# All projections of h ahead of the retention, by seven block products for eight, with results kept in DRAM and low halves made by adding DMAs

## The chip, the cores and the metric

The kernel runs on one core of a Trainium2 chip. The metric is the device time in microseconds of one execution; lower is better. Engine names are those of the profile: PE (TensorE, matmuls), DVE (VectorE), ACT (ScalarE), POOL (GpSimd), SP (SyncE, which here issues nearly all DMAs).

## The reference, cut to what matters

One decoder layer for 1024 tokens of width 1024, batch 1, depth 1, all in f32:

```
mod = c @ w_ada + b_ada;  shift, scale, gate = split(mod, 3)
h = rmsnorm(x, pre_norm_g) * (1 + scale) + shift
q, k, v, z_ret, u_val, u_gate, z_conv, g_a, g_b = split(h @ w_in)   # 1024, 1024, 2048, 2048, then five of 1024
q, k = rotary(q), rotary(k) / 16                                    # 4 heads of 256
ret = head_groupnorm(retention_chunkwise(q, k, v))                  # 4 heads, v of 512 a head, decay per head
y_a = (ret * silu(z_ret)) @ w_ret_out
a = causal_depthwise_conv(u_val * sigmoid(u_gate), 31 taps)
y_b = (silu(layernorm(a)) * silu(z_conv)) @ w_conv_out
y = (sigmoid(g_a) * y_a + sigmoid(g_b) * y_b) @ w_out
out = x + gate * rmsnorm(y, post_norm_g)
```

## The kernel before

**Precision.** Each f32 operand of a large matmul is split into two float32r tiles: hi, a rounded copy made on ACT, and lo = src - hi, made on DVE (`split`, L124). A product is then three matmuls: hi x hi, hi x lo, lo x hi (`mm3`, L142). One matmul is 128 x 128 weights by up to 512 columns; a projection of 256 channels over all tokens (`proj_T` on the two halves of a `load_chunk`) is 2 x 2 tiles x 8 slices of the contraction x 3 = 96 matmuls.

**Block products.** `strassen` (L220) does the same 256 x 1024 x 1024 block with seven products of 12 matmuls, for eight. It needs sums of the weights, which `load_s` (L193) makes on DVE for each block (x1, x2, wa, then splits), and sums of h (T1 to T4), which `sums_of` (L664) makes once. Four copies of PSUM (p1, p5, u2, u3) go through ACT, three sums through DVE, and a callback gets each 128 x 512 result. Weights come through `wst` (two buffers of 512 KB) and their halves through `whl` (three pairs).

**Stages.** First mod, then `make_h` (h transposed to channels x tokens, in hi and lo, 16 tiles). Three `u_chunk`s (u_gate, u_val, plain) store a to DRAM and queue the convolution: 8 x 30 taps on DVE, each over 1024 tokens, put in by `pump` between matmul tiles at a lowered priority (`LATER`). Then q and k of head 0, the last `u_chunk`, and for each head plain q and k projections with the rotary on DVE (`rot_proj`), scores, the v projection token-major (`wide_proj`), states and outputs with a group norm, o kept in DRAM (o_d). After the heads come the sums T1 to T4, beside one plain block of g_a (`PLAIN`), and then block products of z (eight, with o read back and transposed by PE), g_a (three), g_b (four) with the layer norm's statistics, and z_conv (four). Results go to DRAM (r_d, sga_d, sgb_d, b_d). Last, three parts of output projection (two of w_ret, one of w_conv), then w_out, the norm and the residual.

**Order of the work.** The program is unrolled; a scheduler orders each engine's instructions ahead of time, by priority in program order, with its own estimate of durations. At run time each engine's queue, the DMA queue of SP among them, is worked off in order. Buffers come from pools: `unit` (38 tiles of 512 KB), `LD` (three), `TMP` (nine), PSUM (eight banks).

Of the kernel before, what the change touches and what calls it, by code (L numbers as in the profile page):

```python
# [26 lines left out]
PLAIN = 1  # L27
# [42 lines left out]
def block_kernel(ctx: ExitStack, tc: tile.TileContext, x, c, positions, w_ada, w_in, w_ret_out, w_conv_out,  # L70
# [68 lines left out]
    def load_chunk(w, c0, half=0):
        return [load_w(w, half + i, c0 // 256) for i in range(2)]  # L140
# [8 lines left out]
    def proj_T(ch, src, cb, th, name):  # L149
        ps = PS(name)  # L150
        pairs = []
        for k in range(4 * len(ch)):
            hi, lo = ch[k // 4]
            cs = slice(cb * P, cb * P + P)
            ts = slice(th * 512, th * 512 + 512)
            pairs.append(((hi[:, k % 4, cs], lo[:, k % 4, cs]), (src[k][0][:, ts], src[k][1][:, ts])))
        mm3(ps, pairs, True, True)
        return ps

    def load_wide(w, c0, qk):  # L160
        hi, lo = load_w(w, qk % 2, c0 // 256 + qk // 2)
        return [t.rearrange("p (k x) n -> p k (x n)", x=2) for t in (hi, lo)]
# [18 lines left out]
    def proj_group(ch, src, tiles, name):  # L181
        pss = [PS(name) for _ in tiles]
        for k in range(KK):
            hi, lo = ch[k // 4]
            for ps, (cb, th) in zip(pss, tiles):
                cs = slice(cb * P, cb * P + P)
                ts = slice(th * 512, th * 512 + 512)
                mm3(ps, [((hi[:, k % 4, cs], lo[:, k % 4, cs]), (src[k][0][:, ts], src[k][1][:, ts]))],
                    k == 0, k == KK - 1)
        return pss  # L190


    def load_s(w, ci):  # L193
        st = []
        for half in range(2):
            st.append(wst.tile([P, 4, 256], F32, name="ws", tag="ws"))
            nc.sync.dma_start(out=st[half], in_=w[ci, half])
        n0, n1 = slice(0, P), slice(P, 256)
        a11, a21, a12, a22 = st[0][:, :, n0], st[0][:, :, n1], st[1][:, :, n0], st[1][:, :, n1]
        wa = wst.tile([P, 2, 4, P], F32R, name="wa", tag="wa", bufs=1)  # L200
        split(a11, wa[:, 0], wa[:, 1], V)
        x1 = LD("x1").rearrange("p (k n) -> p k n", n=256)
        V.tensor_tensor(out=x1[:, :, n0], in0=a21, in1=a22, op=ALU.add)
        V.tensor_tensor(out=x1[:, :, n1], in0=x1[:, :, n0], in1=a11, op=ALU.subtract)
        x2 = LD("x2").rearrange("p (k n) -> p k n", n=256)
        V.tensor_tensor(out=x2[:, :, n0], in0=a12, in1=x1[:, :, n1], op=ALU.subtract)
        V.tensor_tensor(out=x2[:, :, n1], in0=a11, in1=a21, op=ALU.subtract)
        res = []
        for x in (x1, x2, st[1]):
            hi = whl.tile([P, 4, 256], F32R, name="wh", tag="wh")  # L210
            lo = whl.tile([P, 4, 256], F32R, name="wl", tag="wl")
            split(x, hi, lo, V)
            res.append((hi, lo))
        sets = {"11": (wa[:, 0], wa[:, 1])}
        for names, (hi, lo) in zip((("S1", "S2"), ("S4", "S3"), ("12", "22")), res):
            for j, name in enumerate(names):
                sets[name] = (hi[:, :, j * P:(j + 1) * P], lo[:, :, j * P:(j + 1) * P])
# [65 lines left out]
    wg0 = load_chunk(w_in, UG0)  # L283
# [65 lines left out]
    cout_d = [dram.tile([P, 1024], F32, name=f"cout_d{i}") for i in range(8)]  # L349
    a_d = [dram.tile([P, 1024], F32, name=f"a_d{i}") for i in range(8)]  # L350
    csum_d = dram.tile([P, 1024], F32, name="csum_d")
    mb_d = [dram.tile([P, 1024], F32, name=f"mb_d{i}") for i in range(8)]
    r_d = [dram.tile([P, 1024], F32, name=f"r_d{i}") for i in range(16)]
    csum = U(name="csum")

    ln_tasks = []

    def conv_tasks(i):
# [16 lines left out]
        def end():  # L375
            nc.sync.dma_start(out=cout_d[i], in_=st["o"])
            if i == 0:
                V.tensor_copy(out=csum, in_=st["o"])
            else:
                V.tensor_tensor(out=csum, in0=csum, in1=st["o"], op=ALU.add)  # L380

        bgq.append((1.0, begin))
        for s_ in range(1, CW):
            bgq.append((1.7, lambda s_=s_: tap(s_)))
        bgq.append((0.0, end))
        if i == 7:
            bgq.append((0.0, lambda: nc.sync.dma_start(out=csum_d, in_=csum)))
# [37 lines left out]
    def trig_begin():  # L425
        posi = U(I32, name="posi")
# [40 lines left out]
    bgp.append((4.0, trig_begin))  # L467
    for j, (src, n, red) in enumerate((("a1", 0, 1), ("a1", 1, 1), ("a2", 0, 1), ("a1", 2, 0), ("a2", 1, 0),
                                       ("a1", 3, 0), ("a2", 2, 0))):
        bgp.append((3.5 if red else 1.2, lambda src=src, n=n, red=red, j=j: turns(src, n, red, j == 0)))  # L470
# [3 lines left out]
    def u_chunk(ci):  # L474
        wg = load_chunk(w_in, UG0 + 256 * ci) if ci else wg0
        sg = {}
        for th in range(2):
            if ci == 0:
                make_h(th)
            pss = proj_group(wg, hT, [(0, th), (1, th)], "pg") if ci == 0 else None  # L480
            for cb in range(2):
                ps = pss[cb] if ci == 0 else proj_T(wg, hT, cb, th, "pg")
                sg[cb, th] = TMP(name="sg")
                A.activation(out=sg[cb, th], in_=ps, func=AF.Sigmoid)
                if ci or (cb and th):
                    pump(5.0, 4.0)
        wv = load_chunk(w_in, UV0 + 256 * ci)
        for cb in range(2):
            a = U(name="a")
            for th in range(2):  # L490
                ps = proj_T(wv, hT, cb, th, "pu")
                V.tensor_tensor(out=a[:, th * 512:(th + 1) * 512], in0=ps, in1=sg[cb, th], op=ALU.mult)
                pump(4.4, 4.0)
            nc.sync.dma_start(out=a_d[2 * ci + cb], in_=a)
            conv_tasks(2 * ci + cb)

    for ci in range(3):
        u_chunk(ci)
    while "cos" not in tr:
        pump(0.0, 5.0)  # L500
    sinT, cosT = tr["sin"], tr["cos"]


    def rot_proj(h, c0):
        ch = load_chunk(w_in, c0 + 256 * h)
        res, kf = [], []
        for th in range(2):
            sl = slice(th * 512, (th + 1) * 512)
            p1 = proj_T(ch, hT, 0, th, "pq1")
            p2 = proj_T(ch, hT, 1, th, "pq2")  # L510
            t_a, t_b, t_c, t_d = TMP(name="ta"), TMP(name="tb"), TMP(name="tcc"), TMP(name="td")
            if c0 == K0:
                kf.append(U(F32, (P, 2, 512), "kf"))
                f_a, f_c = kf[th][:, 0, :], kf[th][:, 1, :]
            else:
                f_a, f_c = t_a, t_c
            V.tensor_tensor(out=t_a, in0=p1, in1=cosT[:, sl], op=ALU.mult)
            V.tensor_tensor(out=t_c, in0=p1, in1=sinT[:, sl], op=ALU.mult)
            V.tensor_tensor(out=t_b, in0=p2, in1=sinT[:, sl], op=ALU.mult)
            V.tensor_tensor(out=t_d, in0=p2, in1=cosT[:, sl], op=ALU.mult)  # L520
            V.tensor_tensor(out=f_a, in0=t_a, in1=t_b, op=ALU.subtract)
            V.tensor_tensor(out=f_c, in0=t_c, in1=t_d, op=ALU.add)
            hi = U(F32R, (P, 2, 512), "qkh")
            lo = U(F32R, (P, 2, 512), "qkl")
            split(f_a, hi[:, 0, :], lo[:, 0, :], V)
            split(f_c, hi[:, 1, :], lo[:, 1, :], V)
            res.append((hi, lo))
            pump(3.8, 3.0)
        return (res, kf) if kf else res

    qk0 = (rot_proj(0, Q0), rot_proj(0, K0))
    u_chunk(3)

    o_d = [dram.tile([P, 8, 512], F32, name=f"o_d{i}") for i in range(H)]
    for h in range(H):
        q, kT = (rot_proj(h, Q0), rot_proj(h, K0)) if h else qk0
        kT, kf = kT

        kna = (U(F32R, (P, 4, 256), "knh"), U(F32R, (P, 4, 256), "knl"))
        knb = U(F32R, (P, 4, 256), "knx")  # L540
        kn = [(kna[0][:, t, :], kna[1][:, t, :]) if t < 4 else (knb[:, t - 4, :], knb[:, t - 2, :]) for t in range(6)]
# [415 lines left out]
```

## Time and profile before

| | us |
|---|---|
| median of 3 runs | 1488.21 (1486.33 to 1491.5) |
| the profiled execution | 1492.43 |
| its span | 1490.7 |
| PE busy | 1447.0 |
| DVE busy | 1045.2 |
| ACT busy | 466.1 |
| POOL busy | 48.6 |

The span runs from the first to the last instruction of the profiled execution; the rest of its time lies around it. Busy times are of one engine each and overlap one another. A matmul's recorded duration overlaps that of the next, since the engine is pipelined: the distance between starts is what one costs. The granted clock (PEclk) is TensorE's share of its full 2.4 GHz in a stretch.

### The profile page before, as it was taken

To read this page: it belongs to the slowest core of one execution; us is meant where nothing else is said; L and a number is where in the kernel's file an instruction comes from. 1 tells how busy PE (TensorE), PEld (TensorE's weight loads), DVE (VectorE), ACT (ScalarE), POOL (GpSimd) and SP (SyncE) were. 2 spreads that over 40 slices of the span, in tenths; PEclk is the share of its full clock that TensorE was granted. 3 is DMA by queue.
4 is the path that set the end of the run, shared out by engine and by line. 5 is a ranking of instruction groups with operands and counts; after the bars stand their busy time and mean duration, and the time that the engine had idled before them with its cause. 6 is when DMAs were issued, how large, how long until landed. Compare 5 with 4: busy or idle time off the path is not lost.

```text
span 1490.7 us, 16850 instructions
## 1 busy us (share of the span) xinstructions
PE 1447.0 (97%) x6648; PEld 1193.9 (80%) x6648; DVE 1045.2 (70%) x1374; ACT 466.1 (31%) x696; POOL 48.6 (3%) x69
## 2 busy tenths in 40 slices
PE   6799999999999999999899999999899999999998
PEld 2688888888888888888688888888688888888888
DVE  5869899998697688589889855497955244464335
ACT  2612112132223213222543434454744021122121
POOL 2200000001001001000000000000000000000001
PEclk9899999999999999999899999999999999999999
DMA  9122222212102202121454533466636344353402
GB/s 370 58 100 84 72 71 85 85 57 85 57 29 99 71 29 86 44 70 43 171 171 143 185 97 104 149 205 199 216 124 237 107 160 152 112 190 121 154 29 114
DMA packets 61665, 176.39 MB, mean 118 GB/s; under 512 B 6417, under 2 KB 14737, under 8 KB 61586
## 3 DMA queue, kind: packets, MB, share of 16 engines
q1 hardware_dynamic: 61298, 175.14, 34.8%
q8 instruction: 52, 0.85, 0.2%
q14 instruction: 27, 0.22, 0.0%
q10 hardware_dynamic: 288, 0.17, 0.0%
HBM read 132.30 MB, written 42.99 MB: 118 GB/s over the span
## 4 chain that ended last, share of the span: by engine, by line
PE 87%; DVE 8%; DMA 2%; issue 1%; ACT 1%; POOL 0%; SPq 0%; DVEq 0%; POOLq 0%; ACTq 0%
PE pya L145 6%; PE pya L146 6%; PE pya L147 6%; PE pza L226 6%; PE pq L145 4%; PE pq L147 4%; PE pq L146 4%; PE pv L147 3%; PE pv L145 3%; PE pv L146 3%; PE pzc L226 3%; PE pgaa L226 2%; PE pzca L226 2%; PE py L145 2%; PE py L146 2%; PE py L147 2%
## 5 line engine op out<-in xcount | busy, mean ns | idle before, releaser
L371 DVE SCALAR_TENSOR_TENSOR co<-ca,vec,co 128x1023 f32<-128x1023 f32 (+16 forms) x240 | 303.0, 1266 | 3.6
L125 ACT CAST wh<-ws 128x1024 fp32r<-128x1024 f32 x101 | 106.3, 1052 | 374.7 <-PE pya L146 119.3
L126 DVE TENSOR_TENSOR wl<-ws,wh 128x1024 fp32r<-128x1024 f32 x97 | 118.4, 1222 | 102.6 <-ACT wh L125 99.4
L146 PE MATMUL pya<-rl,wh 128*128 128x512 f32 x384 | 149.4, 390 | 0.0
L145 PE MATMUL pya<-rh,wh 128*128 128x512 f32 x384 | 149.0, 391 | 0.0
L147 PE MATMUL pya<-rh,wl 128*128 128x512 f32 x384 | 148.5, 390 | 0.0
L146 PE MATMUL pv<-wl,hh 128*128 128x512 f32 x256 | 99.8, 390 | 0.0
L147 PE MATMUL pv<-wh,hl 128*128 128x512 f32 x256 | 99.8, 392 | 0.0
L146 PE MATMUL pq<-hl,wh 128*128 128x512 f32 x256 | 99.7, 390 | 0.0
L145 PE MATMUL pq<-hh,wh 128*128 128x512 f32 x256 | 99.7, 390 | 0.0
L145 PE MATMUL pv<-wh,hh 128*128 128x512 f32 x256 | 99.4, 390 | 0.0
L147 PE MATMUL pq<-hh,wl 128*128 128x512 f32 x256 | 99.1, 390 | 0.0
L145 PEld LDWEIGHTS pya<-rh,wh 128*128 128x128 f32 x384 | 72.1, 188 | 15.1 <-ACT wh L125 0.2
L146 PEld LDWEIGHTS pya<-rl,wh 128*128 128x128 f32 x384 | 72.1, 188 | 15.1 <-issue 0.2
L147 PEld LDWEIGHTS pya<-rh,wl 128*128 128x128 f32 x384 | 72.1, 188 | 15.0
L146 PE MATMUL py<-wl,mh 128*128 128x256 f32 (+1 forms) x192 | 61.0, 319 | 0.0
L147 PE MATMUL py<-wh,ml 128*128 128x256 f32 (+1 forms) x192 | 61.0, 319 | 0.0
L145 PE MATMUL py<-wh,mh 128*128 128x256 f32 (+1 forms) x192 | 60.6, 319 | 0.0
L226 PE MATMUL pza<-T,wh 128*128 128x512 f32 x192 | 60.2, 395 | 0.0
L852 DVE TENSOR_TENSOR ya<-pya,gld 128x512 f32<-128x512 f32 x32 | 22.1, 690 | 53.9 <-PE pya L147 53.9
L147 PEld LDWEIGHTS pq<-hh,wl 128*128 128x128 f32 x256 | 48.1, 188 | 10.0
L145 PEld LDWEIGHTS pq<-hh,wh 128*128 128x128 f32 x256 | 48.1, 188 | 9.9
(338 smaller groups left out, 3181.0 us busy)
## 6 DMA issues: line engine op xcount, KB each, us to landing
ws<-in_w_in SPq DMA_DIRECT2D x88, 512.0 KB, 3.6
ada<-in_w_ada SPq DMA_DIRECT2D x16, 512.0 KB, 10.2
o_d<-o SPq DMA_DIRECT2D x16, 512.0 KB, 2.6
oc<-o_d SPq DMA_DIRECT2D x16, 512.0 KB, 5.3
ws<-in_w_ret_out SPq DMA_DIRECT2D x16, 512.0 KB, 4.4
rld<-r_d SPq DMA_DIRECT2D x16, 512.0 KB, 4.6
gld<-sga_d SPq DMA_DIRECT2D x16, 512.0 KB, 4.2
x<-in_x SPq DMA_DIRECT2D x8, 512.0 KB, 10.2
```

The costliest lines, as they stand in the source:

```text
L125: A.copy(out=hi, in_=src)
L126: lo_eng.tensor_tensor(out=lo, in0=src, in1=f(hi), op=ALU.subtract)
L145: T.matmul(ps, a[0], b[0], start=start and i == 0, stop=False)
L146: T.matmul(ps, a[0], b[1], start=False, stop=False)
L147: T.matmul(ps, a[1], b[0], start=False, stop=stop and i == n - 1)
L226: T.matmul(ps, l_[:, k, :], r_, start=start and k == 0 and i == 0, stop=k == 3 and i == 2, skip_group_check=True)
L371: V.scalar_tensor_tensor(out=st["o"][:, s_:], in0=st["a"][:, 0:1024 - s_], scalar=vec[:, i, ROW_CW + k:ROW_CW + k + 1], in1=st["o"][:, s_: ...
L852: V.tensor_tensor(out=y, in0=ps, in1=gld[:, sl], op=ALU.mult)
```

## The change

All 44 blocks of h @ w_in but the first of u_gate and u_val go through `strassen`, in one stage ahead of everything else; `sums_of` therefore runs right after h. q, k (after the rotary), v, silu(z) and the gates are stored in DRAM (q_d, k_d, v_d, sz_d, sga_d, sgb_d). v comes out channels x tokens. The convolution's taps, angles and layer norm are pumped between the products. Retention follows in 16 steps (4 heads x 4 chunks of 256 tokens): `fetch` reads a chunk's q, k and v, splits them and transposes k and v by PE, one step ahead; `scores`, `state` and `outputs` hold the same matmuls as before; `gated` transposes o, multiplies by silu(z) and stores r_d. Between the steps stand the 16 tiles of y_b (`conv_out`, 24 matmuls each), which were the third part of the output projection. The two parts of w_ret stay at the end.

Most low halves of weights are now made by `split_dma`: ACT writes hi and then lo = -hi, and a DMA from POOL's queue adds the source to lo, from DRAM again or from the tile in SBUF. `split` on DVE stays for x2, for what is read back, and for plain blocks. The convolution's sum over channels (csum) is made by adding DMAs in DRAM. Weights are laid out by the host so that blocks are contiguous. `whl` has four pairs for three, `unit` 36 for 38. In the first step `make_h` does the second half of the tokens first.

```diff
-    unit = ctx.enter_context(tc.tile_pool(name="unit", bufs=38))
+    unit = ctx.enter_context(tc.tile_pool(name="unit", bufs=36))
     wst = ctx.enter_context(tc.tile_pool(name="wst", bufs=2))
-    whl = ctx.enter_context(tc.tile_pool(name="whl", bufs=3))
+    whl = ctx.enter_context(tc.tile_pool(name="whl", bufs=4))
...
+    def split_dma(src, hi, lo, again):
+        A.copy(out=hi, in_=src)
+        A.activation(out=lo, in_=f(hi), func=AF.Copy, scale=-1.0)
+        G.dma_start(out=lo, in_=again, accum_op=ALU.add)
...
-        split(a11, wa[:, 0], wa[:, 1], V)
...
+        split_dma(a11, wa[:, b0], wa[:, b1], w[ci, 0][:, b0])
...
+        for names, x, again in ((("S1", "S2"), x1, x1), (("S4", "S3"), x2, None), (("12", "22"), st[1], w[ci, 1])):
+            hi = whl.tile([P, 1024], F32R, name="wh", tag="wh")
+            lo = whl.tile([P, 1024], F32R, name="wl", tag="wl")
+            if again is None:
+                split(x, hi, lo, V)
+            else:
+                split_dma(x, hi, lo, again)
...
             if i == 0:
-                V.tensor_copy(out=csum, in_=st["o"])
+                G.dma_start(out=csum_d, in_=st["o"])
             else:
-                V.tensor_tensor(out=csum, in0=csum, in1=st["o"], op=ALU.add)
+                G.dma_start(out=csum_d, in_=st["o"], accum_op=ALU.add)
...
+    sg = [U(name="sg") for _ in range(2)]
+    for th in (1, 0):
+        make_h(th)
+        pss = proj_group(wg0, hT, [(0, th), (1, th)], "pg")
         for cb in range(2):
...
+            evac_pg(sg)(cb, th, pss[cb], None)
...
+    wv0 = load_chunk(w_in, UV0 // 256)
     for k in range(4):
         sums_of(k)
...
+    for th in (1, 0):
+        for cb in range(2):
+            evac_pu(0, sg)(cb, th, proj_T(wv0, hT, cb, th, "pu"), TMP(name="pu"))
...
+    ws_ = load_s(w_in, UG0 // 256 + 1)
     for k in range(4):
         split(t1s[k // 2][:, k % 2, :], *hT2["T1"][k], V)
...
+    def qk_group(h, c0, dst):
+        ws_ = load_s(w_in, c0 // 256 + h)
+        outs = {}
...
+            if cb == 0:
+                o = outs[th] = U(F32, (P, 2, 512), "qk")
+                V.tensor_tensor(out=o[:, 0, :], in0=src, in1=tr["cos"][:, sl], op=ALU.mult)
+                V.tensor_tensor(out=o[:, 1, :], in0=src, in1=tr["sin"][:, sl], op=ALU.mult)
+                return
+            o = outs[th]
+            t1 = TMP(name="rt")
+            V.tensor_tensor(out=t1, in0=src, in1=tr["sin"][:, sl], op=ALU.mult)
+            V.tensor_tensor(out=o[:, 0, :], in0=o[:, 0, :], in1=t1, op=ALU.subtract)
+            V.tensor_tensor(out=t, in0=src, in1=tr["cos"][:, sl], op=ALU.mult)
+            V.tensor_tensor(out=o[:, 1, :], in0=o[:, 1, :], in1=t, op=ALU.add)
+            nc.sync.dma_start(out=dst[h][:, :, sl], in_=o)
...
+        strassen(ws_, hT2, "pq", evac, lambda: pump(0.6, 0.6))
...
+    u_groups(1, ws_)
+    u_groups(2)
+    u_groups(3)
...
     for h in range(H):
...
+        qk_group(h, Q0, q_d)
+        g_group(GA0, h, sga_d)
+        qk_group(h, K0, k_d)
+        g_group(GB0, h, sgb_d)
+        for cv in range(2):
+            v_group(h, cv)
+        if h < 2:
+            for cz in range(2):
+                z_group(h, cz)
+    for cz in range(2):
+        z_group(2, cz)
+    pump(1e9, 1e9)
...
+    bgp.append((3.5, ln_rstd))
+    bgp.append((2.0, ln_spread))
+    for i in range(2):
+        bgp.append((1.0, lambda i=i: b_load(i)))
+    for cz in range(2):
+        z_group(3, cz)
     pump(1e9, 1e9)
...
+    def fetch(s):
+        h, n = s // NCH, s % NCH
...
+        split(raw, d["hi"], d["lo"], V)
...
+        vh, vl = U(F32R, (P, 2, 512), "vh"), U(F32R, (P, 2, 512), "vl")
+        for b in range(2):
+            ps = PS("vt")
+            for e in range(4):
+                T.transpose(ps[:, e * P:(e + 1) * P], vr[:, e, b * P:(b + 1) * P], ident)
...
+    def conv_out(j):
+        th, ci, cb = j // 8, (j % 8) // 2, j % 2
+        if cb == 0:
+            wc["ch"] = load_chunk(w_conv, ci, by_dma=True)
...
+        mm3(ps, pairs, True, True)
+        V.tensor_tensor(out=t, in0=ps, in1=t, op=ALU.mult)
+        nc.sync.dma_start(out=mb_d[2 * ci + cb][:, halves[th]], in_=t)
...
+    fetch(0)
+    for s in range(NS + 1):
+        if s < NS:
+            scores(s)
+            if s + 1 < NS:
+                fetch(s + 1)
+            if s % NCH < NCH - 1:
+                state(s)
+        if s in (0, 8):
+            for pr in range(4):
+                load_b(s // 8, pr)
+        if s:
+            gated(s - 1)
+        if s < NS:
+            outputs(s)
+            conv_out(s)
```

## Rows read from the trace of the kernel before

**Rows 1.** The page, part 1: busy us, share of the span, instructions.

```profile
PE 1447.0 (97%) x6648; PEld 1193.9 (80%) x6648; DVE 1045.2 (70%) x1374; ACT 466.1 (31%) x696; POOL 48.6 (3%) x69
```

**Rows 2.** The chain of waits by time: start us, us, what, matmuls.

```profile
806.79 2.72 PE pzc L226 x12
809.51 0.87 PE otp L714 x8
```

**Rows 3.** Windows: busy us (instructions) by engine, clock, DMA share, GB/s.

```profile
core 0: us, PE busy (x) PEld busy (x) DVE busy (x) ACT busy (x) POOL busy (x), PEclk, DMA share, GB/s
0.00:37.00 37.00, 25.02 (x68) 11.02 (x68) 18.42 (x30) 7.97 (x11) 7.86 (x21) 1.00 0.95 371
...
75.00:280.00 205.00, 205.00 (x936) 171.02 (x935) 179.57 (x182) 41.30 (x55) 2.40 (x1) 1.00 0.26 86
...
317.00:440.00 123.00, 121.54 (x565) 101.19 (x564) 101.60 (x149) 34.01 (x57) 5.31 (x8) 1.00 0.18 60
...
765.00:905.00 140.00, 140.00 (x673) 116.58 (x672) 109.14 (x132) 55.21 (x81) 0.00 (x0) 1.00 0.46 145
```

**Rows 4.** Windows of PE alone around its two stops: busy us, clock, DMA.

```profile
700.00:740.00 40.00, 33.69 (x149) 0.96 0.40 144
740.00:780.00 40.00, 39.04 (x175) 0.91 0.62 187
...
1050.00:1075.00 25.00, 19.95 (x84) 0.99 0.49 164
1075.00:1100.00 25.00, 24.19 (x95) 0.87 0.32 117
```

**Rows 5.** Timeline of DVE in z's block products: start us, us, instruction.

```profile
799.58 1.23 DVE L126 TENSOR_TENSOR wl<-x,wh 128x1024 fp32r<-128x1024 f32 x1
800.71 0.69 DVE L715 TENSOR_TENSOR u<-u,otp 128x512 f32<-128x512 f32 x1
801.31 1.27 DVE L371 SCALAR_TENSOR_TENSOR co<-ca,vec,co 128x1007 f32<-128x1007 f32 x1
802.49 0.69 DVE L247 TENSOR_TENSOR u<-u,p 128x512 f32<-128x512 f32 x1
```

**Rows 6.** Groups of instructions, shapes apart: busy us, mean ns, idle before.

```profile
L125 ACT CAST wh<-ws 128x1024 fp32r<-128x1024 f32 x101 | 106.3, 1052 | 374.7 <-PE pya L146 119.3 <-PE pu L146 53.5 <-PE pv L147 48.8
...
L647 POOL TENSOR_TENSOR rr<-rr,cst 128x1 f32<-128x1 f32 x32 | 23.6, 746 | 610.7 <-DVE rr L646 610.2
...
L125 ACT CAST wa<-ws 128x512 fp32r<-128x512 f32 x19 | 11.8, 622 | 2.9 <-DMA ws<-in_w_in 1.9 <-PE pgba L226 0.9
...
L232 ACT COPY u<-pza 128x512 f32<-128x512 f32 x16 | 9.4, 585 | 22.3 <-PE pza L226 22.3
```

**Rows 7.** DMA issues: size of one, median us to landing.

```profile
ws<-in_w_in SPq DMA_DIRECT2D x88, 512.0 KB, 3.6
ada<-in_w_ada SPq DMA_DIRECT2D x16, 512.0 KB, 10.2
...
gada<-in_w_ada SPq DMA_DIRECT2D x8, 512.0 KB, 5.2
...
rld<-b_d SPq DMA_DIRECT2D x8, 512.0 KB, 3.9
...
b_d<-p SPq DMA_DIRECT2D x8, 256.0 KB, 4.3
```

**Rows 8.** Timeline of POOL and DVE while POOL makes low halves.

```profile
35.19 5.09 POOL L126 TENSOR_TENSOR wl<-ws,wh 128x1024 fp32r<-128x1024 f32 x2
...
38.01 2.30 DVE L319 TENSOR_TENSOR Bv<-mod,vec 128x4 f32<-128x4 f32 x1
...
40.94 0.17 DVE L319 TENSOR_TENSOR Bv<-mod,vec 128x4 f32<-128x4 f32 x1
```

**Rows 9.** Waits of PE: us in total, times, longest.

```profile
PE pzc L226 <- ACT wh L125: 7.3, 1, 7.3
...
PE pzcc L226 <- ACT p L232: 1.4, 1, 1.4
```

More of the change, by code (lines that the diff above doesn't have):

```diff
@@ L203, in load_s @@
[L203 to L213, printed above, removed]
@@ new lines, in load_s @@
+        x2 = LD("x2")
+        V.tensor_tensor(out=x2[:, b0], in0=a12, in1=x1[:, b1], op=ALU.subtract)
+        V.tensor_tensor(out=x2[:, b1], in0=a11, in1=a21, op=ALU.subtract)
+        aa = blocks(wa)
+        sets = {"11": (aa[:, 0], aa[:, 1])}
+        for names, x, again in ((("S1", "S2"), x1, x1), (("S4", "S3"), x2, None), (("12", "22"), st[1], w[ci, 1])):
+            hi = whl.tile([P, 1024], F32R, name="wh", tag="wh")
+            lo = whl.tile([P, 1024], F32R, name="wl", tag="wl")
+            if again is None:
+                split(x, hi, lo, V)
+            else:
+                split_dma(x, hi, lo, again)
+            hi, lo = blocks(hi), blocks(lo)
@@ L471, in block_kernel @@
     bgp.append((5.0, trig_end))
[L474 to L487, printed above, removed]
-        for cb in range(2):
[L489 to L529, printed above, removed]
@@ new lines, in g_group, with evac, v_group @@
+    def g_group(c0, ci, dst):
+        ws_ = load_s(w_in, c0 // 256 + ci)
+        def evac(cb, th, src, t):
+            A.activation(out=t, in_=src, func=AF.Sigmoid)
+            nc.sync.dma_start(out=dst[2 * ci + cb][:, halves[th]], in_=t)
+        strassen(ws_, hT2, "pga", evac, lambda: pump(1.75, 1.75))
+    def v_group(h, cv):
+        ws_ = load_s(w_in, (V0 + 512 * h) // 256 + cv)
+        def evac(cb, th, src, t):
+            if src is not t:
+                A.copy(out=t, in_=src)
+            nc.sync.dma_start(out=v_d[h][:, 2 * cv + cb, halves[th]], in_=t)
+        strassen(ws_, hT2, "pv", evac, lambda: pump(1.75, 1.75))
@@ new lines, in z_group, with evac @@
+    def z_group(h, cz):
+        ws_ = load_s(w_in, (ZR0 + 512 * h) // 256 + cz)
+        def evac(cb, th, src, t):
+            A.activation(out=t, in_=src, func=AF.Silu)
+            nc.sync.dma_start(out=sz_d[h][:, 2 * cz + cb, halves[th]], in_=t)
+        strassen(ws_, hT2, "pz", evac, lambda: pump(1.75, 1.75))
+    u_groups(1, ws_)
+    u_groups(2)
+    u_groups(3)
+    while "cos" not in tr:
+        pump(0.0, 5.0)
+    for h in range(H):
+        qk_group(h, Q0, q_d)
[7 more added lines that the diff above has]
+                z_group(h, cz)
@@ L723, in block_kernel @@
     rstd = U(name="rstd")
-    csum2 = U(name="csum2")
+    v8 = const.tile([P, 8], F32, name="v8")
     def ln_stats():
-        nc.sync.dma_start(out=csum2, in_=csum_d)
+        csum = U(name="csum")
+        nc.sync.dma_start(out=csum, in_=csum_d)
         for th in range(2):
             ps = PS("mean")
-            T.matmul(ps, ones, csum2[:, th * 512:(th + 1) * 512], start=True, stop=True)
-            A.activation(out=mean[:, th * 512:(th + 1) * 512], in_=ps, func=AF.Copy, scale=1.0 / D)
+            T.matmul(ps, ones, csum[:, halves[th]], start=True, stop=True)
+            A.activation(out=mean[:, halves[th]], in_=ps, func=AF.Copy, scale=1.0 / D)
     def ln_sq(i):
@@ L748, in ln_rstd @@
             ps = PS("var")
-            sl = slice(th * 512, (th + 1) * 512)
-            T.matmul(ps, ones, sqs[:, sl], start=True, stop=True)
+            T.matmul(ps, ones, sqs[:, halves[th]], start=True, stop=True)
             md = TMP(F32, (P, 4, P), "vdiag")
@@ new lines, in state @@
+    def state(s):
+        h, n = s // NCH, s % NCH
+        d = hs_[s]
+        gC = GAMMA[h] ** C
+        if n == 0:
+            s32s[h] = U(F32, (P, 2, 512), "s32")
+        s32 = s32s[h]
+        Sh, Sl = Sn[s + 1] = (U(F32R, (P, 2, 512), "Sh"), U(F32R, (P, 2, 512), "Sl"))
+        for hf in range(2):
+            ps = PS("st")
+            hsl = slice(hf * P, (hf + 1) * P)
+            mm3(ps, [((d["kn"][b][0][:, hsl], d["kn"][b][1][:, hsl]), (d["v"][0][:, b, :], d["v"][1][:, b, :]))
+                     for b in range(2)], True, True)
+            if n == 0:
+                A.copy(out=s32[:, hf, :], in_=ps)
+            else:
+                V.scalar_tensor_tensor(out=s32[:, hf, :], in0=s32[:, hf, :], scalar=gC, in1=ps,
+                                       op0=ALU.mult, op1=ALU.add)
+            A.activation(out=Sh[:, hf, :], in_=s32[:, hf, :], func=AF.Copy, scale=gC)
+            V.scalar_tensor_tensor(out=Sl[:, hf, :], in0=s32[:, hf, :], scalar=gC, in1=f(Sh[:, hf, :]),
+                                   op0=ALU.mult, op1=ALU.subtract)
@@ L824, in load_r @@
         return hi, lo
+    for k in range(KK):
+        bgp.append((2.7, lambda k=k: gate_task(k)))
+    bgp.append((2.7, gate_end))
     order = [(0, 0), (0, 1), (1, 0), (1, 1)]
     gpost = None
[L828 to L833 removed]
+    for part in range(2):
+        rT = [load_r(r_d[8 * part + e]) for e in range(3)]
+        ch0 = load_chunk(w_ret, 0, half=2 * part)
+        rT += [load_r(r_d[8 * part + e]) for e in range(3, 8)]
         for ci in range(4):
[L835 to L836 removed]
+            ch = load_chunk(w_ret, ci, half=2 * part) if ci else ch0
+            if part == 1 and ci == 2:
                 gpost = gate_rows()
```

456 lines of the change are left out of this document (208 added, 248 removed).

## Prediction

> **What bounds the kernel now.** I read the page's busy times first. TensorE (PE) is busy 1447.0 of 1490.7 us and no other engine above 1045 [rows 1]. Busy is not yet peak, so I went to the chain of waits and the timeline for the rate: a block product of 12 matmuls of 512 columns takes 2.72 us, 0.2267 us each, and the plain projections of 75 to 280 fit 936 matmuls, a few of them short, into 205 us, 0.219 each [rows 2, 3]. An instruction's own 0.39 us overlaps its neighbours. So a matmul left out is worth 0.2267 us as long as TensorE does not run dry. The windows say where it runs dry: not at all in 75 to 280 and 765 to 905, by 1.5 us in head 0's retention, 317 to 440 [rows 3], and in two stops, around 735 and 1055, which the clock makes dearer (granted 0.91 and 0.87 of full afterwards) [rows 4]. The kernel is bound by TensorE's instruction count, and two kinds of price matter: matmuls removed or added, and places where TensorE must wait.
>
> **TensorE's work.** A 256-channel block over all tokens is 96 matmuls plain and 7 x 12 = 84 by block products. w_in has 44 such blocks. Before, 19 go by products (8 of z, 3 of g_a, 4 of g_b, 4 of z_conv); after, all but the first of u_gate and of u_val, 42. That removes 23 x 12 = 276 matmuls: -276 x 0.2267 = **-62.6 us**. Added: v now comes out channel-major, and each of 16 retention steps transposes it in 8 pieces. The same transposes on o take 0.87 us for 8 [rows 2], so 16 x 0.87 = **+13.9 us**. Scores, states, outputs, w_conv, w_ret and w_out keep their matmuls, k and o their transposes.
>
> **Cover in the projection stage.** What else is added lies beside TensorE, and the question is whether the others fit. A product block lasts 84 x 0.2267 = 19.04 us. VectorE (DVE) starts a 512-column tensor_tensor each 0.60 us, a 1024-column one each 1.13, a convolution tap each 1.18 [rows 5]; the longer durations overlap. Per block it keeps four sums of weights, one low half and three sums of products: 7 x 0.60 + 1.13 = 5.3 us. Over the 36 product blocks up to the end of z's head 2 (36 x 19.04 = 685 us): 36 x 5.3 = 192; 240 taps x 1.18 = 283; eight convolution beginnings 6; rotary 8 blocks x 12 x 0.60 = 58; u_val products 7; the angles about 25 (an estimate, some 25 passes of 0.6 to 1.2). Sum 571 us, 83% of 685. In 75 to 280 VectorE was busy 179.57 of 205 us, 88%, and TensorE never stopped [rows 3], so this much is covered. ScalarE (ACT): per block seven passes over weights (two of 512, five of 1024 columns), four copies of products, four activations: 2 x 0.62 + 5 x 1.05 + 4 x 0.59 + 4 x 0.62 = 11.3 us of 19 by its groups [rows 6], 60%, against 55.21 of 140 before [rows 3]. Its copies of p1, p5, u2 and u3 are due one product (2.72 us) after they become possible, and the queue is in order; behind a late VectorE sum a late copy stops TensorE. I take **+6 us** (bounds 0 and 40, the rival below).
>
> **The adding DMAs.** No adding DMA and no DMA from GpSimd's (POOL) queue is in the trace. There are three a block, 126, plus 16 for w_conv and 8 on csum_d. Their nearest rows are half-megabyte transfers from SyncE's queue: median 3.6 us for w_in, 5.2 beside a busy stretch, 10.2 when 14 were queued at once [rows 7]. A second read of the addend's target makes the low end unlikely, the queue of 14 the high end; I take 5.2. Three one after another are then 15.6 us, inside 19.04, between 10.8 and 30.6 by the bounds. The result is due late: whl has four pairs, a block uses three, and pair j of the next block waits only for pair j-1 of this one, freed at 8.2 and 13.6 us of a block, while it is needed 19 us later. wa (one buffer) is free after the first product and wanted 16.3 us later. So 5 us of landing is hidden; cost 0. On POOL's queue each waits for ACT's two passes, and behind it stand only other adding DMAs and, in the retention, the 0.75 us power for a group norm [rows 6]. SyncE's queue keeps two loads and at most four stores a block, as in 765 to 905.
>
> GpSimd and VectorE disturb each other in this trace: while GpSimd made a low half, a 4-column VectorE pass took 2.30 us, which takes 0.17 undisturbed [rows 8]. The Trainium skill (SBUF — State Buffer, "Who interferes with whom") has the two share a port pair, and says that descriptors of GpSimd's DMAs wait while VectorE runs a two-port mode, but that tensor_tensor does not hold them off. By that page the taps and sums would leave the DMAs alone and the sum stays; by the rows' 2.1 us for each DMA it would be the second rival. The same skill's page DMA: Bandwidth & Descriptors ("Anatomy of one DMA — SWDGE (gpsimd) path") gives 2.0 us plus bytes at 436 GB/s, an estimate of 3.2 us for 512 KB; by it three take 9.6 us and nothing changes in the sum.
>
> **The start.** make_h(1) goes first, and its x tiles are the last loaded; but h waits for Bv, ready at 41.1 us [rows 8], and the DMAs were at 0.95 share only up to 37 [rows 3]. One square, power and scale are about 2 us. I take 0 (bounds -5, since the second half no longer comes late, and +4). Then the sums T1 to T4 move here. VectorE's work between h and the second product: sums 4 x (2 x 1.13 + 7 x 0.60) = 25.8, T1 2.4, u_val's low halves 2.3, its products 2.4, load_s 5.3: 38.2 us. TensorE has 96 plain matmuls, 21.8 us, and one product, 2.7. It would stop 13.7 us; some sums fit beside u_gate's second half, so 10, and 5 of low clock as around 735 (40 x 0.04 + 40 x 0.09 [rows 4]): 15. That stop replaces the one at 735, where a weight's high half came 7.3 us late [rows 9], and the two windows lost 6.3 + 1.0 busy and 5.2 of clock: 12.5. **+3 us** (-8 to +10).
>
> **Layer norm.** The stop at 1055 cost 5.1 + 0.8 of busy time and 0.13 x 25 + 0.01 x 25 = 3.5 of clock [rows 4], 9.4. There the b tiles' passes crowded VectorE; now six of the eight are spread over the z_conv blocks, but the statistics (16 x 1.13 and some 7) fall, with 10.6 more, into two z blocks, 36 us of VectorE beside 38. I give back **-6** (0 to -9.4).
>
> **Into the retention.** The first y_b tile needs all of b: the last store 4.3, its load 3.9 [rows 7], a pass on ACT 1.05 and on VectorE 1.13, 10.4 us. TensorE has step 0 meanwhile: states 2.7, outputs 2.0, 24 transposes 2.6, scores near 1.5, 8.8. A gap of 2 and a dip of the clock as after 1055: **+7** (0 to 12).
>
> **Retention.** Per step TensorE has 237 / 16 = 14.8 us (432 + 384 matmuls of 512 columns 185, 304 transposes 33, 192 score matmuls near 19); VectorE about 10 and ACT 8, estimates from [rows 5, 6]. Loads are fetched a step ahead; score masks come back after some 3 us, beside 5 us of transposes and states; the norm beside the y_b tile's 5.4. Before, a head lost 1.5. With 16 smaller steps I take 8 for 4.5: **+4** (0 to 25). The y_a parts read r_d of heads 0 and 1 first, long stored: 0.
>
> **Sum.** -62.6 + 13.9 + 6 + 0 + 3 - 6 + 7 + 4 = **-34.7 us**. The profiled execution took 1492.4 us (span 1490.7), 4.2 above the median 1488.2; so span 1456, its time 1458, and against the median **1454 us**.
>
> **Rivals.**
> 1. *As summed*, 1432 to 1475. For it: both kinds of stretch with VectorE packed and TensorE full.
> 2. *GpSimd's DMAs block VectorE.* Place: the 36 blocks; price 2.1 us for each of 108 DMAs, 227 us. 571 + 227 = 798 against 685, +113: 1567 us, slower. It decides once a DMA costs VectorE over 114 / 108 = 1.06 us, and is slower than before from (114 + 35) / 108 = 1.4. Against it: what blocks in [rows 8] is a whole pass of GpSimd over SBUF, and a DMA is no such pass.
> 3. *Adding DMAs too slow.* If they run singly at over 6.3 us, blocks follow them: at 7 us, 42 x (21 - 19.04) = +82, 1536; even with before at 6.6.
> 4. *Late copies on ACT.* 0.8 us a block over 42 blocks eats the gain: about 1488, no change. For it: one wait of 1.4 us for a copy of p in z_conv's blocks [rows 9]; against it, the full stretch 765 to 905.
> 5. *Retention bound by latency.* At 3 us lost a step, 48 instead of 4: 1498, slower. Against it: all its chains have other work beside them.
>
> **How the numbers follow.** Chances: 1: 0.70; 2: 0.08; 3: 0.06; 4: 0.08; 5: 0.08. This kernel's runs spread about 0.3%, 4.5 us, so that is the limit of "same". Rival 4 falls evenly on the three sides: faster 0.73, same 0.06, slower 0.21 (2, 3, 5 and some of 4). The range 1432 to 1500 leaves out 2 and 3 (0.14) and a few hundredths below; likeliest alone 1432 to 1475.
>
> **What would show it.** In the profile after: 6500 TensorE matmuls (6648 - 276 + 128); product blocks 19.0 us apart with TensorE full; a stop near 90 to 105 us and no stop at 735; VectorE near 83% up to the end of head 2; adding DMAs that land within 10 us. Wrong would be: TensorE's chain passing through VectorE taps or POOL in the projection stage, blocks over 20 us, or gaps of microseconds in each retention step.

## The result, and the profile after

The changed kernel takes 1648.6 us (median of 4 runs, 1646.27 to 1652.36) against 1489.62 for the kernel before beside it: a ratio of 1.107 (95% interval 1.104 to 1.111). The forecast was 1454 us, range 1432 to 1500. The profiled execution has a span of 1644.1 us, 188 above the forecast span of 1456.

First the page, parts 1 and 2, of the changed kernel; it answers to [rows 1].

```profile
PE 1445.4 (88%) x6500; PEld 1187.0 (72%) x6500; DVE 1040.1 (63%) x1417; ACT 680.8 (41%) x976; POOL 169.3 (10%) x217
...
PE   5889999999999999999969966585657579999998
...
PEclk9899999999999999999979987787878789999999
```

The 6500 matmuls are as forecast, 148 fewer than before, and yet PE is busy just as long, because a matmul costs nearly twice as much (0.43 us for 0.23, below) where the granted clock falls. Slices are 41.1 us. From the fourth (123 us) they are full, up to a hole at 822 us, in z of head 3; ten broken slices from 945 to 1356 are the retention. After it the tail is full again. Windows of the same trace, columns as in [rows 3], give the stages:

```profile
100.00:140.00 40.00, 35.32 (x148) 28.47 (x147) 36.61 (x44) 23.09 (x31) 6.07 (x7) 0.96 0.76 176
...
100.00:808.00 708.00, 695.27 (x3030) 569.38 (x3028) 584.12 (x676) 355.58 (x488) 102.37 (x118) 1.00 0.77 190
808.00:876.00 68.00, 50.28 (x181) 38.23 (x180) 41.94 (x47) 37.80 (x48) 7.23 (x7) 0.85 0.89 275
876.00:950.00 74.00, 73.67 (x333) 60.64 (x332) 33.16 (x46) 45.47 (x64) 9.44 (x11) 1.00 0.83 219
...
965.00:1377.00 412.00, 279.34 (x1301) 234.50 (x1300) 172.53 (x343) 132.98 (x202) 28.42 (x44) 0.81 0.49 143
```

The last row runs from the first state product (965.1 us) to the last transposes of o (1376.5): 411 us, where the forecast had 237 + 4. PE idles 133 of them at a mean granted clock of 0.81. What it waits for, in the view of PE's waits from 950 to 1380 (line numbers are those of the changed kernel: L719 transposes k into the PSUM tile kn, L727 transposes v into vt, both in `fetch`; the numbers are us in total, times, longest):

```profile
PE kn L719 <- DMA qkr<-k_d: 80.9, 11, 12.3
PE vt L727 <- DMA vr<-v_d: 57.5, 15, 13.8
```

Two rows hold all but 2 of the 140 us that PE idles there: 138 us for loads that were to be there a step ahead, 132 of them from 965 on. Why they are late stands in the chain of waits from 1056 to 1075 and in SyncE's timeline of the same step:

```profile
1056.62 0.70 DVE yb L849
1057.34 0.32 SPq L850
1057.75 0.38 SPq L136
1058.19 0.49 SPq L842
1058.72 1.65 SPq L708
1060.41 0.72 SPq L709
1061.17 9.86 DMA vr<-v_d
1071.17 1.94 PE vt L727 x8
1073.11 0.43 PE st L155
...
1075.33 0.23 PE st L155
```

```profile
1057.34 0.32 SPq L850 DMA_DIRECT2D mb_d<-yb  x1
1057.75 0.38 SPq L136 DMA_DIRECT2D ws<-in_w_conv_out  x1
1058.19 0.49 SPq L842 DMA_DIRECT2D yb<-sgb_d  x1
1058.72 1.65 SPq L708 DMA_DIRECT2D qkr<-q_d  x1
1060.41 0.72 SPq L709 DMA_DIRECT2D qkr<-k_d  x1
1061.17 0.64 SPq L711 DMA_DIRECT2D vr<-v_d  x1
1077.97 1.79 SPq L822 DMA_DIRECT2D r_d<-szl  x4
```

Read them together. The last product of a y_b tile (yb, L849) releases its store (mb_d, L850), and only then does SyncE's queue, in order, come to the next step's loads of q, k and v. So the loads are issued when TensorE has finished the step before. Ahead of their use TensorE has only the scores of the current step; in its own queue the transposes of the fetched chunk stand before state, outputs and the next y_b tile, which need no load. So TensorE stands still for most of a landing in nearly every step, 138 us in 15 steps. After the stop of this step, 11.8 us, it restarts at the lower of its two clock levels: the 8 transposes of v take 1.94 us instead of 0.87 [rows 2], and matmuls start 0.43 us apart and not 0.23 until about 1075.

DMA issues of the changed kernel (size, median us to landing), beside [rows 7]:

```profile
wl<-x POOLq DMA_DIRECT2D x42, 512.0 KB, 5.6
wl<-in_w_in POOLq DMA_DIRECT2D x42, 512.0 KB, 6.3
wa<-in_w_in POOLq DMA_DIRECT2D x42, 256.0 KB, 5.1
...
vr<-v_d SPq DMA_DIRECT2D x16, 512.0 KB, 6.8
...
wl<-in_w_conv_out POOLq DMA_DIRECT2D x16, 512.0 KB, 8.4
```

### The profile page after: what moved, and what is told of

It reads as the page before. It is cut to its first block, busy times and chain, and to the rows that moved or that the text cites. A ratio compares the mean times of both kernels' runs of the same rounds, so it can differ in the third digit from the quotient of the medians.

```text
span 1644.1 us, 17722 instructions
## 1 busy us (share of the span) xinstructions
PE 1445.4 (88%) x6500; PEld 1187.0 (72%) x6500; DVE 1040.1 (63%) x1417; ACT 680.8 (41%) x976; POOL 169.3 (10%) x217
## 4 chain that ended last, share of the span: by engine, by line
PE 72%; DMA 15%; DVE 4%; issue 4%; SPq 2%; ACT 1%; POOL 0%; DVEq 0%; POOLq 0%; ACTq 0%
DMA vr<-v_d 7%; PE pva L236 5%; PE pgaa L236 4%; PE pza L236 4%; PE pya L156 4%; PE pya L157 4%; PE pya L155 3%; PE pqa L236 3%; PE pvc L236 2%; DMA wl<-x 2%; PE pgac L236 2%; PE pzc L236 2%; PE pua L236 2%; PE vt L727 2%; PE py L157 2%
## 5 line engine op out<-in xcount | busy, mean ns | idle before, releaser
L385 DVE SCALAR_TENSOR_TENSOR co<-ca,vec,co 128x1021 f32<-128x1021 f32 (+19 forms) x240 | 302.3, 1265 | 1.4
L129 ACT ACTIVATE wl<-wh 128x1024 fp32r<-128x1024 f32 x100 | 106.2, 1062 | 1.3
L156 PE MATMUL pya<-rl,wh 128*128 128x512 f32 x256 | 99.7, 390 | 0.4 <-DVE rl L125 0.4
L157 PE MATMUL pya<-rh,wl 128*128 128x512 f32 x256 | 99.6, 389 | 0.0
L155 PE MATMUL pya<-rh,wh 128*128 128x512 f32 x256 | 97.3, 391 | 0.0
L719 PE MATMUL kn<-ident,qkr 128*128 128x128 f32 x48 | 12.1, 403 | 80.9 <-DMA qkr<-k_d 80.9
L128 ACT CAST wh<-x 128x1024 fp32r<-128x1024 f32 x42 | 44.2, 1052 | 91.1 <-DVE x L212 52.1
L125 DVE TENSOR_TENSOR wl<-x,wh 128x1024 fp32r<-128x1024 f32 x42 | 51.3, 1222 | 46.9 <-ACT wh L124 46.9
L727 PE MATMUL vt<-ident,vr 128*128 128x128 f32 x128 | 30.2, 414 | 57.5 <-DMA vr<-v_d 57.5
L130 POOL DMA_DIRECT2D wl<-x x42 | 36.5, 870 | 333.3 <-ACT wl L129 144.2
L727 PEld LDWEIGHTS vt<-ident,vr 128*128 128x128 f32 x128 | 24.4, 218 | 61.9 <-issue 58.0
L719 PEld LDWEIGHTS kn<-ident,qkr 128*128 128x128 f32 x48 | 8.1, 204 | 83.2 <-issue 75.4
L130 POOL DMA_DIRECT2D wl<-in_w_in x42 | 36.4, 866 | 304.5 <-ACT wl L129 257.2
```

Source lines behind the costliest of these rows:

```text
L125: lo_eng.tensor_tensor(out=lo, in0=src, in1=f(hi), op=ALU.subtract)
L128: A.copy(out=hi, in_=src)
L129: A.activation(out=lo, in_=f(hi), func=AF.Copy, scale=-1.0)
L130: G.dma_start(out=lo, in_=again, accum_op=ALU.add)
L155: T.matmul(ps, a[0], b[0], start=start and i == 0, stop=False)
L156: T.matmul(ps, a[0], b[1], start=False, stop=False)
```

## The experiments

The kernel before took 1489.36, 1489.29, 1490.28 and 1490.16 us beside the four sets of runs (e1 to e4, e5 to e8, e9 to e11, e12). Theory A was that the loads of the retention are late because of where they stand in SyncE's queue; B, its rival, that they are late because adding DMAs and loads crowd the DMA engines.

**Loads two steps ahead (e1).** The three loads of `fetch` move into a function of their own, issued at the start of a step for the step after next; all else stays.

```diff
...
+    load_qkv(0)
     fetch(0)
+    load_qkv(1)
     for s in range(NS + 1):
         if s < NS:
+            if s + 2 < NS:
+                load_qkv(s + 2)
             scores(s)
...
```

> The loads of q, k and v for step s+2 are issued at the beginning of step s, a whole step before their transposes; nothing else differs. Theory A (each step's loads stand in SyncE's queue behind the store of the y_b tile before, and TensorE's queue has the transposes of step s+1 ahead of step s's own states and outputs, so every step waits for a landing and then runs at the low clock): the 138 us of waits at kn and vt and the low clock after them go, the stretch from 950 to 1375 shrinks from 420 to some 270 us, the whole to about 1500 us. Theory B (the landings themselves are slow, 5 to 10 us, because w_conv is read twice and its low halves are added by DMA beside them, and the DMAs are the limit): the landings stretch further, and it stays above 1600 us.

Measured: 1487.05 us (7 runs), ratio 0.998 (0.996 to 0.999). 162 us came back by moving three loads. PE's waits for these loads shrink from 138 us to 2.8 (L733 is e1's line for the transposes of v), and first state product to last transposes take 262 us (957.2 to 1218.8).

```profile
PE vt L733 <- DMA vr<-v_d: 2.8, 1, 2.8
```

**Transposes later (e2).** The loads stay where they were; the transposes of the fetched chunk, as `turn`, go behind `outputs(s)`, so that states and outputs cover the landing.

```diff
+    def turn(s):
...
             outputs(s)
+            if s + 1 < NS:
+                turn(s + 1)
             conv_out(s)
```

> The loads stay where they are in the program; only the transposes of k and v of step s+1 move behind the outputs of step s, ahead of the y_b tile. Theory A: TensorE has about 8 us of states, transposes of o and outputs while the loads land, so the steps that waited 5 us wait no more and those that waited 10 wait 2 to 4: about 1520 us. Theory B: the same landings, but hidden as well, so it does not tell A from B by itself; with B the landings get longer once steps are shorter, 1580 us.

Measured: 1555.1 us (one run), between A's number and B's, so this run doesn't tell them apart. 51.5 us of waits for k and v remain (23.6 and 27.9): state and outputs of one step are too short a cover.

```profile
PE vt L732 <- DMA vr<-v_d: 27.9, 11, 8.0
PE kn L724 <- DMA qkr<-k_d: 23.6, 7, 6.9
```

**Stores off SyncE's queue (e3).** The stores of r_d and mb_d are issued by POOL.

```diff
-                nc.sync.dma_start(out=r_d[h * 4 + 2 * eh + e][:, cs], in_=sz[:, 2 * eh + e, :])
+                G.dma_start(out=r_d[h * 4 + 2 * eh + e][:, cs], in_=sz[:, 2 * eh + e, :])
...
-        nc.sync.dma_start(out=mb_d[2 * ci + cb][:, halves[th]], in_=t)
+        G.dma_start(out=mb_d[2 * ci + cb][:, halves[th]], in_=t)
```

> The stores of r_d and of the y_b tiles go to GpSimd's queue; SyncE's queue then holds only loads, which wait for nothing but buffers. Theory A: loads are issued as soon as buffers come free, the waits at kn and vt fall from 138 us to under 40, about 1520 us. If the loads are held by buffers and not by the stores ahead of them, it stays within 30 us of 1648.

Measured: 1625.15 us (one run); A's number was missed by 105, and what came is the other case on record, loads held by buffers. The waits in this run's retention, of SyncE's queue and of PE, say why:

```profile
SPq L812 <- DMA r_d<-szl: 170.4, 18, 22.8
```
```profile
PE kn L719 <- DMA qkr<-k_d: 60.5, 10, 12.6
PE vt L727 <- DMA vr<-v_d: 58.8, 14, 13.8
```

With the stores gone, the load of silu(z) (L812) heads the queue. Its pool `LD` has three buffers, so it waits until an r_d store has read one, and the q, k and v loads stand behind it as before. What heads the queue changed; that something waiting stands ahead of the loads did not. The run doesn't contradict A, but alone it would not have shown it.

**No adding DMA in the retention (e4).** `load_chunk(w_conv, ci)` without `by_dma=True`: the low halves of w_conv on VectorE.

> Only the low halves of w_conv are made by VectorE again, so that w_conv is read once and nothing is added by DMA in the retention. Theory A: only the longer landings, those beside a w_conv load, get shorter, by up to 4 us in 8 steps: 1610 to 1640 us. Theory B: landings of 5 us and less, steps of 16 us, about 1520 us.

Measured: 1611.3 us (one run), as A expected. With POOL's 512 KB additions gone, the loads of v land in a median of 6.1 us, for 6.7, and PE still waits 102 us for k and v. The additions and the second read of w_conv that they bring are worth some 37 us, and aren't the main cause.

```profile
PE kn L719 <- DMA qkr<-k_d: 60.8, 11, 8.0
PE vt L727 <- DMA vr<-v_d: 41.4, 15, 9.3
```

**Past one store (e12).** The smallest form of A: the loads stand just ahead of the mb_d store that they stood behind.

```diff
...
     def conv_out(j):
...
         mm3(ps, pairs, True, True)
+        if j + 2 < NS:
+            load_qkv(j + 2)
         V.tensor_tensor(out=t, in0=ps, in1=t, op=ALU.mult)
         nc.sync.dma_start(out=mb_d[2 * ci + cb][:, halves[th]], in_=t)
```

> The changed kernel with one thing moved: the three loads of a retention step's q, k and v stand ahead of the y_b tile's store in SyncE's queue and no longer right behind it; nothing else is fetched earlier. Theory (that store, which waits for the y_b tile's matmuls and product, holds the loads back by about the time of a step's output products and y_b tile, some 10 us, which is what a load takes to land): PE's waits for k and v fall from 138 us to under 40 and the time is 1505 us (1487 to 1525), nearly that of the loads two steps ahead. Rival (the loads are late for more than this store: the r stores ahead of it, or landings that one step cannot hide): the waits stay over 70 us and the time is 1560 to 1640.

Measured: 1526.24 us (4 runs), ratio 1.025 (1.022 to 1.028). PE's waits for the loads from 940 to 1400 us (L725 and L733 are the transposes of k and v):

```profile
PE kn L725 <- DMA qkr<-k_d: 19.2, 5, 5.3
...
PE vt L733 <- DMA vr<-v_d: 5.6, 10, 0.9
```

24.8 us of waits as the theory had it, and a time 1 us above its range. The move is not of one place alone: in the trace the loads now also stand ahead of the load of sgb_d (yb) and, every second step, of those of w_conv, and those of the second chunk are issued ahead of the first step, which brings the first state product forward by 7 us (957.7 for 965.1). In the chain above the store is what they waited for, and the two loads between cost under 1 us. So this move in the queue was worth 122 of the 162 us; the other 39 come with the longer lead of e1.

**What e1 had left.** Windows of e1: the projection stage, the layer norm's stop, the retention.

```profile
100.00:790.00 690.00, 677.65 (x2952) 555.10 (x2951) 577.82 (x668) 346.23 (x474) 99.74 (x115) 0.99 0.77 189
...
790.00:880.00 90.00, 69.78 (x263) 53.38 (x262) 47.94 (x55) 47.63 (x63) 9.86 (x10) 0.87 0.84 253
...
950.00:1210.00 260.00, 251.69 (x1313) 213.70 (x1313) 165.03 (x346) 126.43 (x210) 30.48 (x45) 0.97 0.81 240
```

Four kernels change one of these at a time (the edits of e6 and e7 reach into the layer norm's stretch too), all on top of e1. **Layer norm over four blocks (e5)**: its tasks go to z of heads 2 and 3.

```diff
-    for cz in range(2):
-        z_group(2, cz)
     pump(1e9, 1e9)
...
-        bgp.append((1.0, lambda i=i: ln_sq(i)))
+        bgp.append((4.0, lambda i=i: ln_sq(i)))
...
-    for cz in range(2):
-        z_group(3, cz)
+    for h in (2, 3):
+        for cz in range(2):
+            z_group(h, cz)
```

(The g, v and z blocks pump the taps at 1.9 for 1.75, so that they end ahead of z of head 2.)

> On top of the loads fetched two steps ahead, the layer norm's square sums, h*wf and g/v products are handed out over the blocks of z heads 2 and 3 instead of head 3 alone. Theory (the layer norm's stop is VectorE and ScalarE work that does not fit into two blocks): the stretch of z head 3, which has about 28 us of stop in the run with the loads ahead (PE busy 59.8 of 80 us between 790 and 870 us), loses less than 10, and the time is 1465 us (1455 to 1475). Rival (it waits for the DMAs of the layer norm's inputs, which share queues with the adding DMAs): the stop is spread but stays, 1480 to 1490 us.

**x1's low half on VectorE (e6)**, and **all three of a load step (e7)**:

```diff
-        for names, x, again in ((("S1", "S2"), x1, x1), (("S4", "S3"), x2, None), (("12", "22"), st[1], w[ci, 1])):
+        for names, x, again in ((("S1", "S2"), x1, None), (("S4", "S3"), x2, None), (("12", "22"), st[1], w[ci, 1])):
```

> On top of the loads fetched two steps ahead, the low half of x1 is taken by one VectorE subtraction and no longer by an adding DMA; VectorE gets about 30 us more in the projection stage, some 87 to 90% of it. Theory (the stage's 22 us over its matmul time are waits for adding DMAs that land late): the waits of PE for the low half of x go, 1475 us (1465 to 1482). Rival (the waits are VectorE's order of work, and the adding DMA only ends last by a little): the same time within 4 us, 1483 to 1491.

and, beside it, in e7:

```diff
-        split_dma(a11, wa[:, b0], wa[:, b1], w[ci, 0][:, b0])
+        split(a11, wa[:, b0], wa[:, b1], V)
...
+        for names, x, again in ((("S1", "S2"), x1, None), (("S4", "S3"), x2, None), (("12", "22"), st[1], None)):
```

> On top of the loads fetched two steps ahead, no adding DMA is left in the projection stage: all three low halves of a load step are VectorE subtractions. Theory (VectorE was near its limit and the adding DMAs free about 15% of the stage): VectorE comes to 97% or more of the stage and the time is 1510 us (1495 to 1540). Rival (the adding DMAs cost as much in waits as they free): 1470 to 1490 us.

**w_conv's low halves on VectorE (e8)**, the edit of e4 on top of e1:

> On top of the loads fetched two steps ahead, the low half of w_conv is a VectorE subtraction, so that no adding DMA runs in the retention stage. Theory (once the loads are early enough, what is left of the retention's 20 us over the old stage is the long landings beside w_conv's traffic): 1475 us (1468 to 1483). Rival (what is left is elsewhere, the order of TensorE's own work and the clock): 1484 to 1490 us.

| | us | ratio to before (95%) |
|---|---|---|
| e5 layer norm over four blocks | 1478.7 | 0.9926 (0.9908 to 0.9944) |
| e6 x1's low half on VectorE | 1477.68 | 0.9931 (0.9906 to 0.9956) |
| e7 no adding DMA in the projections | 1477.72 | 0.9912 (0.9886 to 0.9937) |
| e8 none in the retention | 1476.78 | 0.9913 (0.9888 to 0.9938) |

Each is 8 to 10 us below e1's 1487.05 of the first set. The same stretches in their windows: first e5, then e6, e7 and e8.

```profile
790.00:880.00 90.00, 79.88 (x332) 63.02 (x330) 49.06 (x61) 60.01 (x80) 12.99 (x14) 0.96 0.87 250
```
```profile
790.00:880.00 90.00, 73.05 (x285) 55.88 (x286) 54.99 (x63) 49.03 (x65) 6.86 (x7) 0.91 0.77 245
```
```profile
100.00:790.00 690.00, 680.39 (x2981) 557.93 (x2980) 674.02 (x778) 260.51 (x372) 6.03 (x7) 1.00 0.38 122
```
```profile
950.00:1210.00 260.00, 255.70 (x1347) 216.98 (x1346) 185.92 (x368) 118.91 (x201) 19.01 (x32) 0.99 0.66 213
```

e5 gets 69 more matmuls through the layer norm's stretch, but not all of its stop, and it does 30 fewer from 100 to 790 (40 fewer by 600 us, where only its faster taps differ); its time lies between its theory's range and its rival's. e6's size is near its theory's, but its place is not shown: from 100 to 790 us it does 17 matmuls more than e1, but e8, which changes nothing ahead of the retention, does 11 more. PE's waits for low halves of x give way there to waits for those of w_in. Another 22 come in the 90 us of the layer norm, where the DMA share falls from 0.84 to 0.77; that fewer DMAs are the reason is not shown, as e7, with none of the adding ones, does only one matmul more there than e1. e7 refutes its theory: VectorE does 674 of 690 us, 98%, and TensorE still gets 29 matmuls further than in e1. With the taps at this pace the adding DMAs of the projection stage buy nothing. e8 gains 34 matmuls from 950 to 1210 us, where w_conv's loads landed in a median of 11.5 us in e1 and in 5.5 without the additions and the second read of w_conv. First e1, then e8:

```profile
ws<-in_w_conv_out SPq DMA_DIRECT2D x14, 512.0 KB, 11.5
```
```profile
ws<-in_w_conv_out SPq DMA_DIRECT2D x14, 512.0 KB, 5.5
```

**Combinations.** e9 joins e5, e6 and e8; e10 joins e5, e7 and e8; e11 joins e7 and e8.

> Loads two steps ahead, layer norm over four blocks, x1's and w_conv's low halves by VectorE subtractions, the other two adding DMAs of a load step kept. Theory (the three gains of 8 to 10 us lie at different places: the layer norm's stop, the projection blocks, the retention): they add up, 1460 us (1453 to 1467). Rival (they are one gain, less traffic of DMAs in the same stretches): 1472 to 1478 us.

> Loads two steps ahead, layer norm over four blocks and no adding DMA after the first u blocks at all; VectorE some 97% busy in the projection stage. Theory (the adding DMAs bought nothing, and cost their waits): the same as with two of them kept, 1460 us (1453 to 1467). Rival (the layer norm's sums, spread over four blocks, need the VectorE time that the adding DMAs free): 1470 to 1490 us, with PE waiting for VectorE's low halves.

> Loads two steps ahead, no adding DMA after the first u blocks, the layer norm in two blocks as in the changed kernel. The gains at the two places add up: 1468 us (1462 to 1474); if they are one gain: 1476 to 1480 us.

Measured: e9 1455.35 us (5 runs, 0.977, 0.975 to 0.980), e11 1468.26 (0.984, 0.982 to 0.986), e10 1477.82 (0.992, 0.990 to 0.993). The gains of e5, e6 and e8 add up, as those of e7 and e8 do. Those of e5, e7 and e8 don't: e10 takes the time of its rival. It loses ahead of the layer norm, as the windows of e10 and then of e11 show:

```profile
100.00:790.00 690.00, 665.55 (x2884) 543.46 (x2882) 665.98 (x765) 251.10 (x356) 6.84 (x8) 0.99 0.38 122
```
```profile
100.00:790.00 690.00, 680.25 (x2979) 557.42 (x2979) 673.25 (x777) 259.70 (x372) 5.98 (x7) 1.00 0.38 122
```

By 600 us e10 is already 105 matmuls (24 us) behind e11 from 100 on, while its layer norm starts at 798 and the two differ up to there only in the pace of the taps (1.9 for 1.75). From 100 to 790 PE waits 11 us for VectorE's low halves and 11.4 for ACT's high halves, and then 9.2 for the sum over channels (csum). So with VectorE full it is mainly the faster taps that cost; from 790 to 950 us, with the layer norm spread, e10 does 53 matmuls more than e11. A run with the layer norm spread and the taps at 1.75 is missing. e9 beats both kernels. Its windows from 790 to the end of the retention, the last from the first state product to the last transposes of o:

```profile
790.00:946.00 156.00, 149.13 (x654) 121.89 (x652) 93.01 (x116) 90.70 (x128) 12.94 (x14) 0.98 0.77 231
946.00:1192.00 246.00, 244.40 (x1305) 208.01 (x1304) 179.77 (x358) 114.49 (x193) 18.06 (x32) 1.00 0.65 210
```

245 us (946.5 to 1191.5), at the full clock: the forecast's 237 + 4 was close to the price of the retention's work itself. The way there from 411 us was 262 in e1, where the loads of q, k and v are early, and 254 in e8, where w_conv's additions are gone too; why e9 needs another 8 less is not shown.

## Why the prediction was wrong

The step that failed is the one under "Retention", "Loads are fetched a step ahead", with its +4. The program fetches a step ahead; SyncE's queue doesn't. The step named neither the mb_d store and the r_d stores that the loads stand behind, nor what stands behind the transposes in TensorE's own queue. The price is 174 us over the 237 and 7 ahead of the first state. Of the 174, 132 are waits; some 35 are low clock after them, as PE is busy 279 us with what takes it 244 in e9 at the full clock; the rest is what the 237 fell short. e1 and e12 show the cause of nearly all of it, as with early loads 149 of the 174 go; the price of w_conv's additions, put at nothing as well, has up to 8 of what is left (e8). The sign that the prediction named for this case, gaps of microseconds in each retention step, is the one that came. Rival 5, "retention bound by latency", had the place and the sign, but 3 us lost a step where 11 were lost, and its counter-argument, that the chains have other work beside them, was wrong for a queue worked off in order. The terms, against the span:

| term | forecast | measured |
|---|---|---|
| TensorE's count | 6500 | 6500 |
| start | +3 | -5 |
| projection stage | +6 | +16 |
| layer norm | -6 | +20 |
| into the retention | +7 | +7 |
| retention | +4 | +174 |

The differences sum to +198, the span is 188 above the forecast's; 10 us are not located.

- *Start.* By 100 us TensorE had 302 matmuls behind it, before 306; in the next 40 us it does 148, before 178, 6.8 us less. With the 12.5 of [rows 4] gone, that is -5.
- *Projection stage.* 36 blocks in 708 us for 685, of which 7 are counted at the start. VectorE's sum was right: 584 us from 100 to 808 where 571 were counted. The late copies on ACT that the +6 was taken for cost 0.2 us of PE's waits there; 9.5 are for low halves by adding DMAs (the longest 4.5 us, for one of x1) and 2.7 for high halves.
- *Adding DMAs.* 5.1 to 6.3 us in the projection stage, where 5.2 were taken. The Trainium skill's page DMA: Bandwidth & Descriptors ("Anatomy of one DMA — SWDGE (gpsimd) path") gave an estimate of 3.2 us for 512 KB; the measurement is 1.8 to 2 times that. "Cost 0" was too low, by those 9.5 us of waits, and e7 without them gets 29 matmuls, 6.6 us, further. In the retention of e1 they cost 8 to 10 us (e8).
- *GpSimd's DMAs and VectorE (rival 2).* VectorE's 584 us are 13 over the count, with 108 adding DMAs beside them; 2.1 us for each would be 227. The Trainium skill's page SBUF — State Buffer ("Who interferes with whom") has tensor_tensor not stall such DMAs, and DMAs not contend with an engine; VectorE's time in this trace agrees, and whether VectorE ever held a DMA off no run here shows.
- *Layer norm.* 68 us (808 to 876) for two blocks of 38. The term counted VectorE's passes alone. PE waits 7.6 us for the sum of squares and 7.3 for copies on ACT, at a granted clock of 0.85 and a DMA share of 0.89. VectorE is busy 42 of 68 us there, so it is not a lack of VectorE time; the chain of loads, passes and stores in two blocks is the likely cause, and e5 shows that giving it four blocks shortens the stop. How much of it is DMA, and how much the order of work on ACT, stays open.
- *Into the retention.* The size is right by chance: the 7 us from 880 to 965 are waits for k and v of the second chunk, the failed step's, and not for the loads of b, for whose low halves PE waits under 1 us in all.
- *Chances.* Slower was given 0.21, but its own list, rivals 2, 3 and 5 and a third of 4, adds up to 0.25.

With e9, the count of matmuls is worth what was forecast: 1455 us for 1454. That agreement is partly luck, since e9 is another kernel than the one forecast, its projection stage costs more than its term and its start less.

## What to carry to other kernels

"Fetched a step ahead" is a statement about a queue, not about the program: find the last instruction ahead of the load in its own DMA queue, and ask what that one waits for. A load behind a store starts when the store's data is made. And look at the consumer's queue too: work placed behind an operation that needs the load covers nothing. When moving stores to another queue, look at what will head the old one next; a load into a pool of few buffers waits for the stores that empty it.

An operation taken off an engine that still has room is no gain: the adding DMAs freed 96 us of VectorE from 100 to 790 us, and without them e7 is 9 us faster than e1. Whether there is room depends on the rest of the engine's work: with faster taps, e9, which keeps two of the three, is 22 us faster than e10, which keeps none.

## What the runs showed of the hardware

The stops of the retention were paid twice. After a stop of 11.8 us TensorE came back at the lower clock level, 0.43 us from matmul to matmul for 0.23; in the retention of the changed kernel that adds some 35 us to 132 us of waits (busy 279 us for 244 in e9). And beside additions by DMA, other transfers were slower: in the retention of e1 w_conv's loads of 512 KB took a median of 11.5 us, and 5.5 in e8 without the additions and their second read; in the changed kernel, where the same additions are spread over 411 us, all its loads of w_conv took 5.3, and 4.0 without (e4).
